# A second SwiGLU whose gate and up projections are seven block products of sums instead of eight

## The chip, the cores and the metric

One core of a Trainium2 chip runs the kernel. Its engines work side by side, each through its own queue and in that queue's order: TensorE multiplies matrices (PE in the profile, its weight loads PEld), VectorE (DVE) and ScalarE (ACT) do arithmetic on 128 partitions, GpSimd (POOL) does the same more slowly, SyncE (SP) issues transfers from memory. TensorE reads operands in SBUF and writes sums into eight PSUM banks of 128x512 numbers. The metric is the time of one execution in microseconds (us). The kernel before takes 2198.51 us, the median of three runs (2197.66 to 2201.56).

## The reference

Two decoder layers over 1024 tokens of width 1024. Layer 0 mixes tokens with a Conformer convolution, layer 1 with dilated attention; after each mixer stands a SwiGLU block of inner width 2816, and at the end an RMS norm. What the change touches is the second of these lines, in layer 1:

```python
x = x + dilated_attention(h, attn_w_qkv[j], attn_w_o[j], rel_bias)
h = rmsnorm(x, norm_ffn[i])
x = x + swiglu(h, ffn_w_gate[i], ffn_w_up[i], ffn_w_down[i])
# swiglu: (silu(h @ w_gate) * (h @ w_up)) @ w_down, all in float32
```

## The kernel before

Everything is kept transposed: features on the 128 partitions, tokens along the free axis, in two halves of 512 tokens (h = 0 and 1). So `x[d][h]` is feature tile d (8 of them) of one half, 128x512.

A float32 product is made of three products in the chip's faster float32r: each operand is split into a rounded high part and the rest as low part, and `gemm` (line 148) issues, for each of the K tiles of 128 inner features, high x high, low x high and high x low (lines 154 to 156). `split` (line 123) makes the parts: a cast on ScalarE (line 126) and a subtraction on VectorE or GpSimd (line 127). For weights, `weights` (line 137) loads a row of 128x1024 into one of two buffers `ws` and splits it into `wh` and `wl` (three buffers each); in layer 1 the subtraction goes to VectorE for every other row and to GpSimd for the rest (`PATTERNS`).

The SwiGLU of layer 1 is run by `ffn`. It goes through groups of four feature tiles (one group has two) out of 22. `ffn_up` makes, for each tile f, a gate product and an up product for each token half: 8 K tiles, so 24 matmuls, into a PSUM tile `mm`. ScalarE applies Silu to the gate (line 259), VectorE multiplies it with the up product (line 265), and the result is split into the group's hidden tile. `ffn_down` multiplies a group's hidden tiles with the down weights into PSUM tiles `aux` and VectorE adds them to x (line 310). The last group is followed, half by half, by the final norm (`final`).

Into this block leads the hand-over from attention. `attn_layer` ends with two calls of `wo_half` (the output projection, added to x at line 837), each followed by `rms_pair`, which makes the normalised operand of one token half: `rstd` sums the squares of the 8 feature tiles (line 196), TensorE turns the result into a row in PSUM, line 207 multiplies each x tile by it, and the 8 products are split. While the second half's operand is made, `AHEAD[1] = 8` lets TensorE do the first 8 gate and up jobs for half 0 alone; the weights of these jobs are loaded and split a second time for half 1.

The order of the instructions on each engine is fixed when the program is built, by a scheduler that goes by the order of the code and by its own estimate of when operands and buffers are there. Nothing is reordered when it runs: an instruction that waits holds up all behind it on its engine.

## Time and profile before

| | |
|---|---|
| median of three runs | 2198.51 us |
| the profiled execution | 2198.14 us |
| its span on the core | 2196.3 us |
| TensorE busy | 2136.2 us, 97% |
| VectorE busy | 1147.2 us, 52% |
| ScalarE busy | 802.0 us, 37% |
| GpSimd busy | 662.2 us, 30% |
[...]

A matmul's busy time in the profile overlaps with the next one's, so a group's busy time divided by its count (389 ns) is not what one costs; the number of matmuls that start in a window says that. Line numbers of the profile are those of the kernel before; in the changed kernel the same lines stand one further down as far as attention.

### The profile page before, as it was taken

The numbers are of one execution on the slowest core, as the hardware profiler recorded it, in microseconds if no ns is written. First come the engines' busy times: TensorE is split into PE (matmuls) and PEld (weight loads), VectorE is DVE, ScalarE is ACT, GpSimd is POOL, SyncE is SP. The second block draws the span as 40 slices with busy tenths as digits, with TensorE's granted clock in tenths as the row PEclk, the third lists the DMA queues.
The fourth block names the chain that finished last, engine by engine and source line by source line (L and its number), as shares of the span: only waits on it lengthen the run. The fifth ranks groups of instructions, "written<-read, shape, count | busy, mean of one in ns | idle before, by whom it ended". The sixth has DMA issues, their size and how long they took to land.

```text
span 2196.3 us, 24621 instructions
## 1 busy us (share of the span) xinstructions
PE 2136.2 (97%) x9832; PEld 1733.7 (79%) x9832; DVE 1147.2 (52%) x1536; ACT 802.0 (37%) x1226; POOL 662.2 (30%) x384
## 2 busy tenths in 40 slices
PE   8998889999999999999999999999999999999998
PEld 6785677778877788888887877778888888888887
DVE  8998597996463333432743355684423232323225
ACT  7666466423433222212434434453212122211114
POOL 3997189811322122210321111142211111111103
PEclk9999999999999999999999999999999999999999
DMA  6111222222323232321231211123312221212212
GB/s 242 49 39 48 68 68 87 87 96 87 106 77 127 92 98 96 102 70 48 87 106 53 73 63 51 59 89 96 97 57 64 71 67 48 87 48 67 67 48 77
DMA packets 54486, 173.66 MB, mean 79 GB/s; under 512 B 6237, under 2 KB 11620, under 8 KB 54372
## 3 DMA queue, kind: packets, MB, share of 16 engines
q1 hardware_dynamic: 52068, 169.21, 23.5%
q10 hardware_dynamic: 2304, 2.88, 0.4%
q8 instruction: 77, 1.26, 0.2%
q14 instruction: 37, 0.30, 0.0%
HBM read 165.51 MB, written 6.55 MB: 78 GB/s over the span
## 4 chain that ended last, share of the span: by engine, by line
PE 78%; DVE 11%; POOL 6%; ACT 2%; DMA 2%; issue 1%; SPq 0%; DVEq 0%; ACTq 0%; POOLq 0%
PE mm L154 17%; PE mm L155 17%; PE mm L156 17%; PE aux L154 7%; PE aux L155 7%; PE aux L156 7%; POOL ap L398 5%; DVE cacc L406 4%; PE att L735 1%; DVE slot L127 1%; PE aux L773 1%; PE aux L765 1%; DVE wl L127 1%; ACT slot L126 1%; DVE ssq L196 1%
## 5 line engine op out<-in xcount | busy, mean ns | idle before, releaser
L154 PE MATMUL mm<-slot,wh 128*128 128x512 f32 x1888 | 742.1, 393 | 10.1 <-ACT slot L126 8.7
L155 PE MATMUL mm<-slot,wl 128*128 128x512 f32 x1888 | 740.1, 392 | 2.1 <-DVE wl L127 2.1
L156 PE MATMUL mm<-slot,wh 128*128 128x512 f32 x1888 | 736.1, 392 | 1.9 <-DVE slot L127 1.2
L127 POOL TENSOR_TENSOR wl<-ws,wh 128x1024 fp32r<-128x1024 f32 (+1 forms) x135 | 321.3, 2380 | 1335.0 <-ACT wh L126 1298.7
L126 ACT CAST wh<-ws 128x1024 fp32r<-128x1024 f32 (+1 forms) x278 | 288.3, 1038 | 593.1 <-PE aux L156 249.7
L154 PEld LDWEIGHTS mm<-slot,wh 128*128 128x128 f32 x1888 | 356.5, 189 | 91.5 <-ACT slot L126 10.4
L155 PEld LDWEIGHTS mm<-slot,wl 128*128 128x128 f32 x1888 | 356.7, 189 | 79.5 <-DVE wl L127 3.2
L156 PEld LDWEIGHTS mm<-slot,wh 128*128 128x128 f32 x1888 | 355.7, 188 | 78.8 <-DVE slot L127 2.4
L127 DVE TENSOR_TENSOR wl<-ws,wh 128x1024 fp32r<-128x1024 f32 (+1 forms) x143 | 184.1, 1288 | 341.9 <-ACT wh L126 326.4
L398 POOL TENSOR_TENSOR ap<-ap,m 128x512 f32<-128x512 f32 x170 | 248.2, 1493 | 44.3 <-ACT m L397 44.2
L154 PE MATMUL aux<-slot,wh 128*128 128x512 f32 x640 | 251.1, 392 | 8.4 <-DVE x L310 8.4
L155 PE MATMUL aux<-slot,wl 128*128 128x512 f32 x640 | 250.5, 391 | 0.5 <-DVE wl L127 0.5
L156 PE MATMUL aux<-slot,wh 128*128 128x512 f32 x640 | 250.2, 391 | 0.0
L310 DVE TENSOR_TENSOR x<-aux,x 128x512 f32<-128x512 f32 (+1 forms) x200 | 133.0, 668 | 173.6 <-PE aux L156 173.3
L406 DVE SCALAR_TENSOR_TENSOR cacc<-u,wd_sb,cacc 128x512 f32<-128x512 f32 x288 | 200.0, 748 | 0.2
L397 ACT ACTIVATE m<-u,wd_sb 128x512 f32<-128x512 f32 x170 | 121.6, 724 | 90.6 <-POOL ap L398 90.5
L154 PEld LDWEIGHTS aux<-slot,wh 128*128 128x128 f32 x640 | 120.8, 189 | 34.2 <-DVE x L310 9.2
L155 PEld LDWEIGHTS aux<-slot,wl 128*128 128x128 f32 x640 | 121.0, 189 | 26.3 <-DVE wl L127 0.9
L156 PEld LDWEIGHTS aux<-slot,wh 128*128 128x128 f32 x640 | 120.8, 189 | 25.3
L127 DVE TENSOR_TENSOR slot<-tmp,slot 128x512 fp32r<-128x512 f32 x66 | 102.0, 1548 | 34.7 <-ACT slot L126 34.4
L265 DVE TENSOR_TENSOR ftmp<-mm,ftmp 128x512 f32<-128x512 f32 x52 | 36.0, 692 | 151.6 <-PE mm L156 151.5
L154 PE MATMUL mm<-slot 128*128 128x512 f32 x256 | 102.5, 400 | 9.4 <-ACT slot L499 6.7
(174 smaller groups left out, 1923.0 us busy)
## 6 DMA issues: line engine op xcount, KB each, us to landing
ws<-wd SPq DMA_DIRECT2D x84, 512.0 KB, 3.4
ws<-wg SPq DMA_DIRECT2D x66, 512.0 KB, 3.4
ws<-wu SPq DMA_DIRECT2D x66, 512.0 KB, 3.4
ws<-w SPq DMA_DIRECT2D x40, 512.0 KB, 3.5
ws<-wqkv SPq DMA_DIRECT2D x34, 512.0 KB, 3.5
ws<-wo SPq DMA_DIRECT2D x16, 384.0 KB, 3.0
x<-xT SPq DMA_DIRECT2D x16, 256.0 KB, 6.1
scratch<-tmp ACTq DMA_DIRECT2D x12, 192.0 KB, 2.0
```

Source lines behind the costliest of these rows:

```text
L126: a = nc.scalar.copy(hi, src)
L127: b = eng.tensor_tensor(out=lo, in0=src, in1=hi.bitcast(F32), op=ALU.subtract)
L154: nc.tensor.matmul(ps, wh[:, sl], xh, start=(k == 0), stop=False)
L155: nc.tensor.matmul(ps, wl[:, sl], xh, start=False, stop=False)
L156: nc.tensor.matmul(ps, wh[:, sl], xl, start=False, stop=(k == kt - 1))
L196: nc.vector.tensor_tensor(out=acc, in0=acc, in1=sq, op=ALU.add)
L265: nc.vector.tensor_tensor(out=t, in0=ps, in1=s, op=ALU.mult)
L310: nc.vector.tensor_tensor(out=x[d][h][:, sl], in0=ps, in1=x[d][h][:, sl], op=ALU.add)
L397: nc.scalar.activation(m, src(c, k), AF.Copy, scale=wk)
L398: nc.gpsimd.tensor_tensor(out=a, in0=a, in1=m, op=ALU.add)
L406: nc.vector.scalar_tensor_tensor(out=a if k or late else u[h, c][:, :TH], in0=src(c, k), scalar=wk, in1=b if k == nv - 1 else a, op0=ALU.mult,
L735: nc.tensor.matmul(s[a][:, pr, c0:], q[rs, pr, us], kb, start=True, stop=True)
```

## The change

Write the product of a pair of feature tiles with all tokens as a 2x2 block product: the weights have two blocks along the features (i, a tile each) and two along the inner dimension (512 features each, a11, a12, a21, a22), the activations two blocks along the inner dimension and two token halves (b11, b12, b21, b22). The plain way takes eight block products of 4 K tiles, 12 matmuls each. The new function `seven_ffn` makes the four results from seven, whose operands are sums: weights a11, a12, a22, s1 = a21 + a22, s2 = s1 - a11, s3 = a11 - a21 and s4 = a12 - s2, and activations b11, b21, b22, t1 = b12 - b11, t2 = b22 - t1, t3 = b22 - b12 and t4 = b21 - t2. `quad` does this for one pair and one projection. Products that go into one result accumulate in one PSUM tile; a partial sum that two results need is copied or added out of PSUM between (u2, u3), and the sinks add it to the other results. `parts` splits each weight operand of 128x512, with the subtraction always on VectorE, into buffers with the tags `wl` and `wh` in turn.

`first_half` makes b11 and b21 while the second `wo_half` runs; `other_half` makes the five operands that need token half 1. `begin` does, for the first two pairs, the two products that need half 0 alone (`AHEAD[1] = 2`), and keeps the value that `quad` goes on with. `down` is the down projection of one pair, for both halves, and stands between the next pair's gate and up quads. The last two pairs share a down projection as before.

```diff
@@ -66,10 +66,11 @@
-AHEAD = (4, 8)
-
-
-TAIL = (256,)
+AHEAD = (4, 2)
+TAILS = (slice(0, 256), slice(256, 512))
 GROUPS = (
-    ((0, 1, 2, 3), (4, 5, 6, 7), (8, 9), (10, 11, 12, 13), (14, 15, 16, 17), (18, 19, 20, 21)),
+    ((0, 1), (2, 3), (4, 5), (6, 7), (8, 9), (10, 11), (12, 13), (14, 15), (16, 17), (18, 19, 20, 21)),
 )
@@ -878,10 +879,235 @@
             todo.append(partial(merged, 1))
             step(STEPS[8])
             wo_half(0, o[0], partial(step, STEPS[9]))
-            out = [rms_pair(0, V_FFN + DC)]
-            wo_half(1, o[1])
-            out.append(rms_pair(1, V_FFN + DC))
-            return out
+        return partial(wo_half, 1, o[1])
+    def seven_ffn(layer, gcol, second_half, ahead):
+        groups = GROUPS[layer]
+        n_pairs = FT // 2
+        H = D // 2
+        with ExitStack() as cs:
...
+            def hid_tile(dtype=F32R):
+                return fpool.tile([P, 2, TH], dtype, tag="hid", name="hid", bufs=4)
...
+            def sub(out, a, b, eng=nc.vector, op=ALU.subtract):
+                eng.tensor_tensor(out=out, in0=a, in1=b, op=op)
+            X = {}
+            def operand(*names):
+                for n in names:
+                    X[n] = slot([P, 2, 4, TH]) if n != "T3" else fpool.tile([P, 2, 4, TH], F32R, name="T3")
+                    nc.vector.tensor_copy(X[n][:, 0, 0, 0:2], ones[:, 0:2])
+            def into(n, k, src, eng=nc.vector):
+                split(src, X[n][:, 0, k], X[n][:, 1, k], eng)
...
+            def first_half():
+                operand("B11", "B21")
+                bc = rstd(lambda c: x[c][0], TH, main)
+                hold = [hid_tile(F32) for _ in range(4)]
+                for c in range(DC):
+                    t = hold[c % 4][:, c // 4]
+                    normed(t, 0, c, gcol, bc, whole)
+                    into("B21" if c // 4 else "B11", c % 4, t, nc.gpsimd if c % 2 else nc.vector)
+                return hold
+            def other_half(hold):
+                operand("T3", "T2", "T1", "B22", "T4")
+                bc = rstd(lambda c: x[c][1], TH, main)
+                for k in range(4):
+                    b11, b21 = hold[k][:, 0], hold[k][:, 1]
+                    b12, t1, b22, t2 = (tmp() for _ in range(4))
+                    normed(b12, 1, k, gcol, bc, whole)
+                    sub(t1, b12, b11)
+                    normed(b22, 1, 4 + k, gcol, bc, whole)
+                    into("B22", k, b22, nc.gpsimd)
+                    sub(t2, b22, t1)
+                    into("T2", k, t2)
+                    t3, t4 = sum_tile(), sum_tile()
+                    sub(t3, b22, b12)
+                    into("T3", k, t3)
+                    into("T1", k, t1)
+                    sub(t4, b21, t2)
+                    into("T4", k, t4)
+            def sum_tile():
+                return fpool.tile([P, TH], F32, tag="sum", name="sum", bufs=3)
+            def product(ps, w, n, start=True):
+                for k in range(4):
+                    sl = slice(k * P, (k + 1) * P)
+                    wh, wl = w[:, 0, sl], w[:, 1, sl]
+                    xh, xl = X[n][:, 0, k], X[n][:, 1, k]
+                    nc.tensor.matmul(ps, wh, xh, start=start and k == 0, stop=False, skip_group_check=not start)
+                    nc.tensor.matmul(ps, wl, xh, start=False, stop=False, skip_group_check=not start)
+                    nc.tensor.matmul(ps, wh, xl, start=False, stop=k == 3, skip_group_check=not start)
...
+            def parts(src):
+                turns["operand"] += 1
+                tag = "wl" if turns["operand"] % 2 else "wh"
+                t = wpool.tile([P, 2, H], F32R, tag=tag, name="wp")
+                split(src, t[:, 0], t[:, 1], nc.vector)
+                return t
+            def begin(ap, sink):
+                r = row(ap)
+                b1 = mm_ps()
+                product(b1, parts(r[:, :H]), "B11")
+                keep = s_tile()
+                nc.scalar.copy(keep, b1)
+                product(b1, parts(r[:, H:]), "B21", False)
+                sink(0, 0, b1, None)
+                return keep
+            def quad(row0, row1, sink, kept=None):
+                r0, r1 = row(row0), row(row1)
+                a11, a12, a21, a22 = (r[:, sl] for r in (r0, r1) for sl in (slice(0, H), slice(H, D)))
+                b1, u2 = None, kept
+                if kept is None:
+                    b1 = mm_ps()
+                    product(b1, parts(a11), "B11")
+                    u2 = tmp()
+                    nc.scalar.copy(u2, b1)
+                s1, s2 = sum_tile(), sum_tile()
+                sub(s1, a21, a22, op=ALU.add)
+                sub(s2, s1, a11)
+                b2 = mm_ps()
+                product(b2, parts(s2), "T2")
+                nc.vector.tensor_tensor(out=u2, in0=b2, in1=u2, op=ALU.add)
+                s3 = sum_tile()
+                sub(s3, a11, a21)
+                b4 = mm_ps()
+                product(b4, parts(s3), "T3")
+                u3 = tmp()
+                nc.vector.tensor_tensor(out=u3, in0=b4, in1=u2, op=ALU.add)
+                b3 = nps_ps()
+                product(b3, parts(s1), "T1")
+                sink(1, 1, b3, u3)
+                if b1 is not None:
+                    product(b1, parts(a12), "B21", False)
+                    sink(0, 0, b1, None)
+                product(b4, parts(a22), "T4", False)
+                sink(1, 0, b4, u2)
+                s4 = sum_tile()
+                sub(s4, a12, s2)
+                product(b3, parts(s4), "B22", False)
+                sink(0, 1, b3, u2)
...
+            def up_sink(s, hid, place, first=False):
+                def hidden(i, h):
+                    t = hid[i, h] = place(i, h)
+                    split(s[i, h], t[:, 0], t[:, 1], nc.vector)
+                if first:
+                    hidden(0, 0)
+                def fn(i, h, ps, u):
+                    t = s[i, h]
+                    if u is None:
+                        sub(t, ps, t, op=ALU.mult)
+                    else:
+                        v = tmp()
+                        sub(v, ps, u, op=ALU.add)
+                        sub(t, v, t, op=ALU.mult)
+                    hidden(i, h)
+                return fn
+            def down(p, hid):
+                for b in range(2):
+                    r = row(wd[layer, 2 * p + b])
+                    for j in range(2):
+                        w = parts(r[:, j * H : (j + 1) * H])
+                        for i in range(2):
+                            d = b * 4 + j * 2 + i
+                            for h in range(2):
+                                ps = aux_ps()
+                                gemm(ps, (w[:, 0], w[:, 1]), lambda k: (hid[k, h][:, 0], hid[k, h][:, 1]), 2, i * 2 * P)
+                                sub(x[d][h], ps, x[d][h], op=ALU.add)
+            hold = first_half()
+            second_half()
+            other_half(hold)
+            gates = [dict() for _ in range(n_pairs)]
+            hids = [dict() for _ in range(n_pairs)]
+            kept = {}
+            for p in range(ahead):
+                kept[p, 0] = begin(wg[layer, 2 * p], gate_sink(gates[p]))
+                kept[p, 1] = begin(wu[layer, 2 * p], up_first(gates[p]))
+            for p in range(n_pairs):
+                last = p == n_pairs - 1
+                quad(wg[layer, 2 * p], wg[layer, 2 * p + 1], gate_sink(gates[p]), kept.get((p, 0)))
+                if 0 < p < n_pairs - 1:
+                    down(p - 1, hids[p - 1])
+                place = lambda i, h: hid_tile()
+                if last:
+                    rest = slot([P, 2, 2, 2, TH])
+                    place = lambda i, h: rest[:, i, h]
+                quad(
+                    wu[layer, 2 * p], wu[layer, 2 * p + 1], up_sink(gates[p], hids[p], place, p < ahead), kept.get((p, 1))
+                )
...
     def final(h, sl, sc):
@@ -904,8 +1130,7 @@
     hs = conv_and_half_ffn()
     hs = ffn(0, NHALF, hs, 0, lambda h, sl, sc: rms_pair(h, V_MIX + DC, sc))
-    hs = attn_layer(hs)
-    ffn(1, 0, hs, AHEAD[1], final, [slice(a, b) for a, b in zip((0,) + TAIL, TAIL + (TH,))])
+    seven_ffn(1, V_FFN + DC, attn_layer(hs), AHEAD[1])
```

Two places of VectorE's queue show what moved. The first is the hand-over, from the point where the statistics of token half 1 are there. Before: line 207 makes the normalised tiles `tmp`, line 127 the low parts of the operand (`slot_10651`), of the first hidden tile (`slot_10731`) and of a weight row (`wl`).

```order
L203 RECIPROCAL rs_10684<-sd_10682 128x4
L265 TENSOR_TENSOR ftmp_10797<-mm_10772,ftmp_10764 128x512
L127 TENSOR_TENSOR slot_10731<-ftmp_10797,slot_10731 128x512
L207 SCALAR_TENSOR_TENSOR tmp_10691<-x0_1_87,vec_76,aux_10686 128x512
L207 SCALAR_TENSOR_TENSOR tmp_10695<-x1_1_89,vec_76,aux_10686 128x512
L207 SCALAR_TENSOR_TENSOR tmp_10699<-x2_1_91,vec_76,aux_10686 128x512
L207 SCALAR_TENSOR_TENSOR tmp_10703<-x3_1_93,vec_76,aux_10686 128x512
L127 TENSOR_TENSOR slot_10651<-tmp_10695,slot_10650 128x512
L207 SCALAR_TENSOR_TENSOR tmp_10707<-x4_1_95,vec_76,aux_10686 128x512
L207 SCALAR_TENSOR_TENSOR tmp_10711<-x5_1_97,vec_76,aux_10686 128x512
L127 TENSOR_TENSOR slot_10651<-tmp_10703,slot_10650 128x512
L207 SCALAR_TENSOR_TENSOR tmp_10715<-x6_1_99,vec_76,aux_10686 128x512
```

After: line 208 makes the normalised tiles, line 914 the sums (`tmp`, `sum`) and line 128 the low parts of T1 (`slot_10658`), T2 (`slot_10656`), T3 and T4 (`slot_10662`), `hid` holds b11.

```order
L204 RECIPROCAL rs_10694<-sd_10692 128x4
L128 TENSOR_TENSOR wp_10919<-ws_10899,wp_10919 128x512
L208 SCALAR_TENSOR_TENSOR tmp_10701<-x0_1_87,vec_76,aux_10696 128x512
L914 TENSOR_TENSOR tmp_10702<-tmp_10701,hid_10418 128x512
L208 SCALAR_TENSOR_TENSOR tmp_10703<-x4_1_95,vec_76,aux_10696 128x512
L914 TENSOR_TENSOR tmp_10704<-tmp_10703,tmp_10702 128x512
L914 TENSOR_TENSOR sum_10713<-tmp_10703,tmp_10701 128x512
L128 TENSOR_TENSOR slot_10658<-tmp_10702,slot_10658 128x512
L914 TENSOR_TENSOR sum_10714<-hid_10418,tmp_10704 128x512
L208 SCALAR_TENSOR_TENSOR tmp_10723<-x1_1_89,vec_76,aux_10696 128x512
L128 TENSOR_TENSOR slot_10656<-tmp_10704,slot_10656 128x512
L128 TENSOR_TENSOR T3_10654<-sum_10713,T3_10654 128x512
```

It goes on like this for the four inner tiles, and ends with the first weight operands, `wp_10944` for s2 and `wp_10981` for s1.

```order
L914 TENSOR_TENSOR sum_10939<-ws_10937 128x512
L128 TENSOR_TENSOR slot_10656<-tmp_10770,slot_10656 128x512
L128 TENSOR_TENSOR T3_10654<-sum_10779,T3_10654 128x512
L128 TENSOR_TENSOR slot_10662<-sum_10780,slot_10662 128x512
L914 TENSOR_TENSOR sum_10940<-sum_10939,ws_10935 128x512
L914 TENSOR_TENSOR sum_10960<-ws_10935,ws_10937 128x512
L128 TENSOR_TENSOR wp_10944<-sum_10940,wp_10944 128x512
L128 TENSOR_TENSOR wp_10981<-sum_10939,wp_10981 128x512
```

From the first of line 208 to the low part `wp_10944` stand 47 instructions now, 8 of them of line 208; TensorE's next instruction behind the `begin` products reads `wp_10944`. In the same place the eight of line 207 stood with four low parts on VectorE (the other four on GpSimd).

The second place is the start of a down projection in the middle of the layer. Before, the additions to x (line 310) stand with the low parts of weight rows between them.

```order
L265 TENSOR_TENSOR ftmp_11273<-mm_11248,ftmp_11240 128x512
L127 TENSOR_TENSOR slot_10732<-ftmp_11273,slot_10732 128x512
L310 TENSOR_TENSOR x0_0_86<-aux_11283,x0_0_86 128x512
L310 TENSOR_TENSOR x1_0_88<-aux_11297,x1_0_88 128x512
L127 TENSOR_TENSOR wl_11382<-ws_11379,wh_11381 128x1024
L310 TENSOR_TENSOR x2_0_90<-aux_11317,x2_0_90 128x512
L310 TENSOR_TENSOR x3_0_92<-aux_11331,x3_0_92 128x512
L310 TENSOR_TENSOR x4_0_94<-aux_11351,x4_0_94 128x512
L310 TENSOR_TENSOR x5_0_96<-aux_11365,x5_0_96 128x512
```

After, for a pair in the middle: the down projection's last weight operand (`wp_12615`), the next up quad's first one (`wp_12655`, from the rows `ws_12650` and `ws_12652`), its sums, the ends of the gate quad (`s`), and then the first addition to x.

```order
L128 TENSOR_TENSOR wp_12615<-ws_12578,wp_12615 128x512
L914 TENSOR_TENSOR s_12483<-mm_12414,tmp_12389 128x512
L128 TENSOR_TENSOR wp_12655<-ws_12650,wp_12655 128x512
L914 TENSOR_TENSOR sum_12672<-ws_12652 128x512
L914 TENSOR_TENSOR s_12503<-nps_12432,tmp_12389 128x512
L914 TENSOR_TENSOR sum_12673<-sum_12672,ws_12650 128x512
L914 TENSOR_TENSOR sum_12693<-ws_12650,ws_12652 128x512
L914 TENSOR_TENSOR x0_0_86<-aux_12511,x0_0_86 128x512
L128 TENSOR_TENSOR wp_12677<-sum_12673,wp_12677 128x512
L914 TENSOR_TENSOR x0_1_87<-aux_12519,x0_1_87 128x512
```

The first addition to x now stands behind four instructions that read the up quad's two weight rows. Over one pair in the middle VectorE has 60 instructions of 128x512, 16 for the gate quad, 24 for the up quad and 20 for the down projection.

## Rows read from the trace of the kernel before

**Rows 1.** which engines are busy, over the whole span: engine, busy us (share), instructions
```profile
PE 2136.2 (97%) x9832; PEld 1733.7 (79%) x9832; DVE 1147.2 (52%) x1536; ACT 802.0 (37%) x1226; POOL 662.2 (30%) x384
```

**Rows 2.** the chain that ended last, by engine, over the whole span
```profile
PE 78%; DVE 11%; POOL 6%; ACT 2%; DMA 2%; issue 1%; SPq 0%; DVEq 0%; ACTq 0%; POOLq 0%
```

**Rows 3.** windows in the second layer's SwiGLU: length, then busy us (xcount) per engine
```profile
core 0: us, PE busy (x) PEld busy (x) DVE busy (x) ACT busy (x) POOL busy (x), PEclk, DMA share, GB/s
1500.00:1550.00 50.00, 50.00 (x222) 41.42 (x221) 19.11 (x14) 13.96 (x18) 9.58 (x4) 1.00 0.32 100
1800.00:1850.00 50.00, 50.00 (x223) 41.39 (x222) 13.07 (x12) 10.20 (x14) 4.79 (x2) 1.00 0.17 54
2050.00:2100.00 50.00, 50.00 (x223) 41.39 (x222) 12.24 (x11) 9.72 (x13) 7.18 (x3) 1.00 0.17 53
```

**Rows 4.** groups by line and form, 1500 to 2100 us
```profile
L156 PE MATMUL mm<-slot,wh 128*128 128x512 f32 x595 | 231.5, 389 | 0.0
...
L156 PE MATMUL aux<-slot,wh 128*128 128x512 f32 x288 | 112.0, 389 | 0.0
...
L127 POOL TENSOR_TENSOR wl<-ws,wh 128x1024 fp32r<-128x1024 f32 x39 | 93.4, 2394 | 504.9 <-ACT wh L126 504.9
...
L127 DVE TENSOR_TENSOR slot<-ftmp,slot 128x512 fp32r<-128x512 f32 x38 | 65.2, 1715 | 30.6 <-ACT slot L126 30.6
L310 DVE TENSOR_TENSOR x<-aux,x 128x512 f32<-128x512 f32 x80 | 55.1, 690 | 99.6 <-PE aux L156 99.6
...
L126 ACT CAST slot<-ftmp 128x512 fp32r<-128x512 f32 x37 | 22.8, 616 | 73.4 <-DVE ftmp L265 73.4
L259 ACT ACTIVATE ftmp<-mm 128x512 f32<-128x512 f32 x37 | 22.2, 601 | 157.6 <-PE mm L156 157.6
```

**Rows 5.** VectorE's timeline at the hand-over: start us, us, instruction [idle before]
```profile
1454.78 2.89 DVE L196 TENSOR_TENSOR ssq<-ssq,tmp 128x512 f32<-128x512 f32 x1
1457.59 0.68 DVE L837 TENSOR_TENSOR x<-mm,x 128x512 f32<-128x512 f32 x1
1458.19 0.68 DVE L127 TENSOR_TENSOR slot<-tmp,slot 128x512 fp32r<-128x512 f32 x1
1458.79 1.48 DVE L196 TENSOR_TENSOR ssq<-ssq,tmp 128x512 f32<-128x512 f32 x2
...
1475.06 2.52 DVE L127 TENSOR_TENSOR slot<-ftmp,slot 128x512 fp32r<-128x512 f32 x1 [0.95 <-ACT slot L126]
1477.50 2.71 DVE L207 SCALAR_TENSOR_TENSOR tmp<-x,vec,aux 128x512 f32<-128x512 f32 x4
```

**Rows 6.** GpSimd's timeline in the same stretch
```profile
1453.01 1.30 POOL L127 TENSOR_TENSOR slot<-tmp,slot 128x512 fp32r<-128x512 f32 x1 [1.26 <-ACT slot L126]
1454.26 2.86 POOL L127 TENSOR_TENSOR wl<-ws,wh 128x1024 fp32r<-128x1024 f32 x1
...
1474.64 2.39 POOL L127 TENSOR_TENSOR wl<-ws,wh 128x1024 fp32r<-128x1024 f32 x1 [9.19 <-ACT wh L126]
```

**Rows 7.** what TensorE waited for, 1400 to 2197 us, the longest
```profile
PE mm L155 <- DVE wl L127: 2.1, 1, 2.1
PE mm L176 <- DVE fssq L196: 1.9, 1, 1.9
```

**Rows 8.** windows before, in and after TensorE's short stop (PEclk, then DMA share, GB/s, last)
```profile
1415.00:1420.00 5.00, 3.60 (x14) 1.99 (x13) 4.91 (x8) 2.90 (x5) 1.82 (x1) 1.00 0.25 80
1420.00:1425.00 5.00, 4.99 (x15) 3.44 (x15) 4.67 (x8) 1.28 (x3) 1.46 (x2) 0.66 0.24 79
1430.00:1435.00 5.00, 5.00 (x24) 4.14 (x23) 4.46 (x7) 2.40 (x4) 1.81 (x1) 1.00 0.01 2
```

**Rows 9.** weight loads: queue, count, size, median us from issue to landing
```profile
ws<-wg SPq DMA_DIRECT2D x66, 512.0 KB, 3.4
```

**Rows 10.** TensorE's timeline at the kernel's end
```profile
2187.87 0.60 PE L176 MATMUL mm<-ones,fssq 128*128 128x1 f32 x4 [1.90 <-DVE fssq L196]
```

More of the change, by code (lines that the diff above doesn't have):

```diff
@@ L880, in attn_layer, with f32, nps_ps, s_tile @@
             wo_half(0, o[0], partial(step, STEPS[9]))
-            out = [rms_pair(0, V_FFN + DC)]
-            wo_half(1, o[1])
-            out.append(rms_pair(1, V_FFN + DC))
-            return out
+        return partial(wo_half, 1, o[1])
[4 more added lines that the diff above has]
+        with ExitStack() as cs:
+            nps = cs.enter_context(tc.tile_pool(name="nps", bufs=2, space=PS))
+            fpool = cs.enter_context(tc.tile_pool(name="fpool", bufs=1))
+            turns = {"operand": 0}
+            def f32(ap):
+                return ap.bitcast(F32)
+            def nps_ps():
+                return nps.tile([P, TH], F32, tag="nps", name="nps")
+            def hid_tile(dtype=F32R):
+                return fpool.tile([P, 2, TH], dtype, tag="hid", name="hid", bufs=4)
+            def s_tile():
+                return fpool.tile([P, TH], F32, tag="s", name="s", bufs=6)
+            def sub(out, a, b, eng=nc.vector, op=ALU.subtract):
[7 more added lines that the diff above has]
+                split(src, X[n][:, 0, k], X[n][:, 1, k], eng)
+            whole = slice(0, TH)
+            def first_half():
[35 more added lines that the diff above has]
+                    nc.tensor.matmul(ps, wh, xl, start=False, stop=k == 3, skip_group_check=not start)
+            def row(ap):
+                r = wpool.tile([P, D], F32, tag="ws", name="ws", bufs=2)
+                nc.sync.dma_start(r, ap)
+                return r
+            def parts(src):
[46 more added lines that the diff above has]
+                sink(0, 1, b3, u2)
+            def gate_sink(s):
+                def fn(i, h, ps, u):
+                    t = s[i, h] = s_tile()
+                    if u is None:
+                        nc.scalar.activation(t, ps, AF.Silu)
+                    else:
+                        sub(t, ps, u, op=ALU.add)
+                        nc.scalar.activation(t, t, AF.Silu)
+                return fn
+            def up_first(s):
+                def fn(i, h, ps, u):
+                    sub(s[i, h], ps, s[i, h], op=ALU.mult)
+                return fn
+            def up_sink(s, hid, place, first=False):
[4 more added lines that the diff above has]
+                    hidden(0, 0)
+                def fn(i, h, ps, u):
+                    t = s[i, h]
+                    if u is None:
+                        sub(t, ps, t, op=ALU.mult)
+                    else:
+                        v = tmp()
+                        sub(v, ps, u, op=ALU.add)
+                        sub(t, v, t, op=ALU.mult)
+                    hidden(i, h)
+                return fn
+            def down(p, hid):
[30 more added lines that the diff above has]
+                )
+            gi = len(groups) - 1
+            ws = down_weights(layer, gi)
+            sc = Scratch(tpool, "tmp", fpool, "s", nps_ps)
+            sc.acc = sc.out = s_tile
+            four = {(j, h): hids[n_pairs - 2 + j // 2][j % 2, h] for j in range(4) for h in range(2)}
+            for h in range(2):
+                for sl in TAILS if h else (slice(0, TH),):
+                    for d in range(DC):
+                        ps = aux_ps()[:, : sl.stop - sl.start]
+                        gemm(ps, ws[d // 2], lambda k: (four[k, h][:, 0, sl], four[k, h][:, 1, sl]), 4, d % 2 * 4 * P)
+                        nc.vector.tensor_tensor(out=x[d][h][:, sl], in0=ps, in1=x[d][h][:, sl], op=ALU.add)
+                    final(h, sl, sc)
```

## The prediction

> **What bounds the kernel now.** I read the shares of the engines first. TensorE is busy for 97% of the span, VectorE for 52%, ScalarE for 37%, GpSimd for 30% [rows 1], and the chain that ended last runs through TensorE for 78% [rows 2]. Shares over the whole span hide stages, so I then cut the stage of the change into windows: from 1500 to 2100 us TensorE has no idle time, at the full granted clock, while VectorE is busy for a quarter to two fifths [rows 3]. In this stage time is the number of matmuls times the distance between two starts. The distance is not the 389 ns that a group gives as mean, because neighbours overlap: 3 x 595 + 3 x 288 = 2649 matmuls start in 600 us [rows 4], 0.2265 us each. What TensorE waits for from 1400 us on is little: 2.1 us for a weight's low part in the hand-over from attention and 1.9 us for the last sum of squares [rows 7].
>
> So a matmul less in this stage is 0.2265 us less, as long as the other engines, which get more to do, deliver in time. There are three places to look at: the stage itself, its first microseconds, and its end.
>
> **Matmuls removed.** Gate and up of 22 tiles for two halves were 22 x 2 x 2 x 24 = 2112 matmuls. Now 11 pairs x 2 projections x 7 products x 12 = 1848. The down projection keeps its 1056. That is 264 fewer, all 128x512: 264 x 0.2265 = **59.8 us** less TensorE time.
>
> **VectorE in the middle of the stage.** A pair in the middle gives TensorE 168 + 96 = 264 matmuls, 59.8 us by chance the same number. VectorE has 60 instructions per pair. What one costs depends on GpSimd: undisturbed ones start 0.60 us apart (1457.59, 1458.19, 1458.79) with a duration of 0.68 [rows 5], and those that read PSUM have a mean of 0.69 [rows 4]. Where GpSimd works, an instruction with both inputs in SBUF stands until GpSimd is through: the one of 1454.78 took 2.89 us and ended at 1457.67, just after GpSimd's of 1454.26 ended at 1457.12; the one of 1475.06 took 2.52 us beside GpSimd's of 1474.64 [rows 5, 6]. This makes the 1.715 us of the hidden tile's low part before [rows 4]. The pairs give GpSimd nothing, so I take 0.60 to 0.69: 36 to 41 us of 59.8. ScalarE has 22 casts, 2 copies and 4 Silus per pair, 28 x 0.62 = 17 us [rows 4]. By load both are hidden behind TensorE.
>
> Load is not enough, since VectorE's queue is in order. Its tightest place is the start of a down projection, where the first addition to x frees the PSUM tile that the down projection's fourth result takes (there are three), and stands behind sums of the next two weight rows. Their transfer can be issued only when the down projection's last weight part has been read out of the buffer. From the product whose Silu stands ahead of that cast on ScalarE to the down projection's fourth result TensorE has 54 matmuls, 12.2 us. In it must go: Silu 0.60, cast 0.62, low part 0.60, transfer 3.4 and the second row's issue behind the first's, some 0.3, five VectorE instructions 3.0 [rows 4, 5, 9]: 8.5 us. That leaves 3.7 us, and it is the smallest margin that I count in the pairs. I add nothing for them.
>
> **The hand-over.** Here it doesn't fit. Once the statistics of token half 1 stand in PSUM, the kernel before had 139 of the 192 matmuls of its eight early jobs left, 31.5 us, for eight normalised tiles and their parts. Now 48 of the 96 matmuls of `begin` are left, 48 x 0.2265 = 10.9 us, and then TensorE needs the low part of s2, which is the 47th VectorE instruction. Eight of these are normalisations, four in 2.71 us [rows 5], 8 x 0.68 = 5.4 us. The other 39 cost 39 x 0.60 = 23.4 us. GpSimd makes the four low parts of b22 in this stretch, 1.30 us each [rows 6]; all four in the way would be 5.2 us, none 0, and I take 4.0 because most of the 47 have both inputs in SBUF. Instructions that need the result of the one just ahead may wait a little: two such additions took 1.48 us [rows 5], 0.2 more than two free ones; for some four of them 0.8 us. Sum 33.6 us, minus 10.9: TensorE stands for **22.7 us**. The bounds are 18 (none of the two extras) and 32 (5.2, and 0.2 for each of the 47).
>
> [...]
>
> [...]
>
> Right behind the restart TensorE's second matmul needs the next low part, one VectorE instruction later: **0.6 us**. After that each product of 12 matmuls (2.7 us) needs about two and a half VectorE instructions (1.5 us), so VectorE gets ahead again.
>
> **The end and the rest.** The last group's down projection and the final norm keep their form, with 1.9 us of waiting for the last sum of squares [rows 7, 10]; I add nothing, with 1 us to either side. The weights of the eight early jobs are no longer loaded and split twice. That was off the path.
>
> **Sum.** -59.8 + 22.7 + 2.0 + 0.6 = -34.5. The profiled execution took 2198.14 us (span 2196.3 and 1.8 around it), the median of the runs is 2198.51, 0.4 above. 2198.1 - 34.5 = 2163.6, so **2164 us**. With the bounds of the hand-over alone (18.0 + 0.6 at least, 32 + 4 + 0.6 at most, and 1 for the end) it is 2156 to 2176.
>
> **Rivals.**
> 1. The hand-over is cheaper. If half of its VectorE work were done earlier, the stop would be 33.6 / 2 - 10.9 = 6 us and the time 2198.1 - 59.8 + 6 + 2 = 2146. For it speaks that the stage before has VectorE time to spare. Against it: all 47 instructions need the statistics that TensorE itself puts into PSUM ahead of the 48 matmuls, and the first weight operand stands last in the queue.
> 2. Each pair waits. Two rows of 512 KB are now asked for at once, and the 3.4 us of landing [rows 9] is for rows that came one by one. If both landed 5.7 us later than counted, the margin of 3.7 is gone by 2 us in each of nine pairs: 18 us, 2182. Against it: the transfer engines are busy for 13 to 32% in this stage [rows 3], room for both.
> 3. Slower: VectorE becomes the bound of the pairs. This decides once an instruction takes on average more than (59.8 + 34.5 / 9) / 60 = 1.06 us. At 1.08 a pair takes 64.8 us, nine pairs lose 45, and the time is 2209. For it speak the 1.715 us that a low part takes now [rows 4]; against it, that these stood beside GpSimd's 39 subtractions of 2.394 us, and that none of those is left.
> That the change doesn't do what it says would show as a distance between matmuls other than 0.2265 us; shape and operand layout are the same, and no row speaks for it.
>
> **How the numbers follow.** The forecast has 0.64 and its own range is 2156 to 2176. The cheaper hand-over has 0.09, pairs that wait 0.19 (most of it below 2190, a little within 0.2% of the time before), slower 0.08 with what I have not thought of. The range of 2150 to 2182 leaves out about 0.2: the cheapest hand-overs below, the upper half of rival 2 and rival 3 above. Differences under 0.2%, 4 us, are about what a measurement of this kernel can't tell from none (its three runs span 3.9 us). Faster by more than that 0.90, within 0.03, slower 0.07.
>
> **What would show it.** In the profile after, windows in the middle of the pairs have TensorE at 50 of 50 us with 222 or 223 matmuls, GpSimd at 0 and VectorE near 0.65; matmuls start 0.2265 us apart. At the hand-over TensorE has one wait of about 23 us for a low part `wp`, with a granted clock of about half right behind it, and 47 VectorE instructions from the first normalisation to that low part in about 34 us. No wait of TensorE inside the pairs is above 1 us. If windows of pairs show TensorE idle, rival 2 (a wait for an `aux` tile behind a transfer) or 3 (VectorE at 1.0) holds; if the hand-over's stop is under 15 us or over 33 us, its term is wrong.

## The result: faster by 24.5 us where 34.5 were forecast

The changed kernel takes 2174.7 us (median of 4 runs, 2173.0 to 2177.3) against 2199.2 before (4 runs): ratio 0.9889, 95% interval 0.9872 to 0.9906. The direction is right and the time lies in the range of 2150 to 2182, but ten of the 34.5 us are missing. The profiled execution took 2172.99 us, 25.15 less than the one before.

The page of the kernel after, as [rows 1, 2]: busy us (share) and instructions by engine, then the chain that ended last.

```profile
PE 2087.4 (96%) x9568; PEld 1684.9 (78%) x9568; DVE 1356.6 (62%) x1975; ACT 843.8 (39%) x1360; POOL 559.9 (26%) x340
...
PE 76%; DVE 11%; POOL 6%; issue 3%; ACT 2%; DMA 1%; SPq 0%; POOLq 0%; DVEq 0%; ACTq 0%
```

TensorE has exactly 264 instructions fewer than in [rows 1] and still carries the chain. Now the windows of the pairs, as [rows 3]:

```profile
1550.00:1600.00 50.00, 50.00 (x218) 40.72 (x217) 33.42 (x53) 14.29 (x24) 0.00 (x0) 1.00 0.16 53
1800.00:1850.00 50.00, 50.00 (x220) 40.75 (x219) 32.69 (x51) 15.08 (x25) 0.00 (x0) 1.00 0.17 54
2050.00:2100.00 50.00, 50.00 (x220) 40.93 (x219) 31.91 (x49) 15.05 (x25) 0.00 (x0) 1.00 0.15 52
```

TensorE is busy for all of it at the full granted clock, VectorE for 0.64 to 0.67, GpSimd not at all: as forecast. But 218 to 220 matmuls start in 50 us, not 222 or 223. Each has become 1 to 2% dearer, with no wait to show for it. TensorE's waits from 1400 us on (total, times, longest) hold none inside the pairs. As [rows 7, 10]:

```profile
PE mm L967 <- ACT wp L127: 18.7, 1, 18.7
PE mm L177 <- DVE s L197: 3.6, 2, 3.3
PE mm L967 <- ACT s L990: 2.0, 1, 2.0
PE aux L155 <- DVE x L1109: 1.8, 2, 1.2
PE mm L156 <- DVE wl L128: 1.8, 1, 1.8
```

The first and the third are the hand-over (L967 to L969 are the products' matmuls, `mm` and `nps` their PSUM tiles, L990 is the copy in `begin`), the second and the fourth stand in the last group and the final norm, and the fifth lies before 1470 us, ahead of the hand-over. Behind 2100 us the kernel before had, beside the 1.9 us of [rows 7] and a wait of 0.6 us that both kernels have:

```profile
PE aux L154 <- DVE x L310: 0.3, 1, 0.3
```

**Where the distance grew.** One product on T3 from TensorE's timeline (start us, duration), its first and last matmul:

```profile
1651.40 0.39 PE L967 MATMUL mm<-T,wp 128*128 128x512 f32 x1
...
1653.96 0.40 PE L969 MATMUL mm<-T,wp 128*128 128x512 f32 x1
```

Twelve matmuls have eleven distances: 2.56 / 11 = 0.2327 us. Averaged over the starts of 1560 to 2110 us in the same way, matmuls that stream T3 or a hidden tile stand 0.2333 us apart, those that stream a slot 0.2276. Before, all streamed slots, at 0.2267. The duration (0.39) shows nothing of this. What the slow ones share is the pool: T3 and the hidden tiles lie in `fpool`, all else that the products stream in slots.

**The hand-over.** VectorE's timeline, as [rows 5]: the first normalisation, the four stretched instructions, and the first weight's low part.

```profile
1474.03 0.74 DVE L208 SCALAR_TENSOR_TENSOR tmp<-x,vec,aux 128x512 f32<-128x512 f32 x1
...
1477.41 1.78 DVE L128 TENSOR_TENSOR slot<-tmp,slot 128x512 fp32r<-128x512 f32 x1
...
1487.71 1.10 DVE L128 TENSOR_TENSOR slot<-tmp,slot 128x512 fp32r<-128x512 f32 x1
...
1494.86 1.10 DVE L128 TENSOR_TENSOR slot<-tmp,slot 128x512 fp32r<-128x512 f32 x1
...
1499.55 1.75 DVE L914 TENSOR_TENSOR sum<-tmp 128x512 f32<-128x512 f32 x1
...
1505.65 1.90 DVE L128 TENSOR_TENSOR wp<-sum,wp 128x512 fp32r<-128x512 f32 x3
```

With the first normalisation 46 instructions stand ahead of the low part, which is the 47th; it starts 31.6 us after the first, and forecast were 33.6 for all 47. The stretched ones overlap with GpSimd's four subtractions, which start at 1476.95, 1485.00, 1492.60 and 1499.15 and take 1.60 to 3.26 us. Not every instruction with both inputs in SBUF stood until GpSimd was through: those of 1485.25, 1485.85 and 1486.45 took 0.68 us each beside GpSimd's of 1485.00, which took 3.26. TensorE's timeline shows the two stops and the restart:

```profile
1483.94 0.50 PE L967 MATMUL mm<-slot,wp 128*128 128x512 f32 x1 [1.96 <-ACT s L990]
...
1505.67 0.80 PE L967 MATMUL mm<-slot,wp 128*128 128x512 f32 x1 [18.72 <-ACT wp L127]
1506.26 0.72 PE L967 MATMUL nps<-slot,wp 128*128 128x512 f32 x1
1506.78 0.63 PE L968 MATMUL mm<-slot,wp 128*128 128x512 f32 x1
1507.21 0.63 PE L969 MATMUL mm<-slot,wp 128*128 128x512 f32 x1
...
1510.09 0.39 PE L967 MATMUL mm<-slot,wp 128*128 128x512 f32 x1
1510.31 0.39 PE L968 MATMUL mm<-slot,wp 128*128 128x512 f32 x1
```

The long stop ends with the high part of s2, ScalarE's cast (L127), and not with the low part that the prediction named; the low part is needed one matmul later. After the stop most starts are 0.43 us apart until 1510, then 0.23. The windows around it (granted clock is the third number from the end), as [rows 8]:

```profile
1500.00:1505.00 5.00, 0.00 (x0) 0.00 (x0) 5.00 (x8) 1.50 (x4) 0.75 (x1) 0.50 0.00 0
1505.00:1510.00 5.00, 4.33 (x10) 3.36 (x11) 4.30 (x7) 2.79 (x5) 0.00 (x0) 0.51 0.17 32
1510.00:1515.00 5.00, 5.00 (x23) 4.03 (x23) 2.62 (x4) 0.43 (x1) 0.00 (x0) 1.00 0.44 179
```

The granted clock is 0.50 of full from 1500 to 1505 us, 0.51 from 1505 to 1510 and 1.00 from 1510 on. The ten matmuls from 1505.67 to 1510.09 took 4.42 us, at 0.2267 they would have taken 2.27.

ScalarE's timeline shows where the first stop came from, the 1.96 us before 1483.94, and what the cast at the end of the long one waited for:

```profile
1482.30 0.62 ACT L127 CAST hid<-s 128x512 fp32r<-128x512 f32 x1 [1.84 <-DVE s L914]
1482.82 0.59 ACT L1033 ACTIVATE s<-mm 128x512 f32<-128x512 f32 x1
1483.31 0.58 ACT L990 COPY s<-mm 128x512 f32<-128x512 f32 x1
...
1505.00 1.66 ACT L127 CAST wp<-sum 128x512 fp32r<-128x512 f32 x3 [2.45 <-DVE sum L914]
```

The copy that TensorE waits for first stands in ScalarE's queue behind a cast that waits for a product of VectorE. The cast at 1505.00 starts right behind VectorE's sum for s2 (1504.23, 0.68 us), after 2.45 us in which ScalarE had nothing to do: both stops go back to VectorE's queue.

### The profile page after: what moved, and what is told of

Read it like the earlier page. It is cut to its first block, busy times and chain, and to the rows that moved or that the text cites. A ratio compares the mean times of both kernels' runs of the same rounds, so it can differ in the third digit from the quotient of the medians.

```text
span 2171.2 us, 24611 instructions
## 1 busy us (share of the span) xinstructions
PE 2087.4 (96%) x9568; PEld 1684.9 (78%) x9568; DVE 1356.6 (62%) x1975; ACT 843.8 (39%) x1360; POOL 559.9 (26%) x340
## 4 chain that ended last, share of the span: by engine, by line
PE 76%; DVE 11%; POOL 6%; issue 3%; ACT 2%; DMA 1%; SPq 0%; POOLq 0%; DVEq 0%; ACTq 0%
PE mm L155 11%; PE mm L156 11%; PE mm L157 11%; PE aux L155 6%; PE aux L157 6%; PE aux L156 6%; POOL ap L399 5%; PE mm L967 4%; PE mm L968 4%; PE mm L969 4%; DVE cacc L407 4%; PE nps L967 2%; PE nps L968 2%; PE nps L969 2%; DVE slot L128 2%
## 5 line engine op out<-in xcount | busy, mean ns | idle before, releaser
L155 PE MATMUL mm<-slot,wh 128*128 128x512 f32 x1184 | 468.5, 396 | 10.1 <-ACT slot L127 8.7
L156 PE MATMUL mm<-slot,wl 128*128 128x512 f32 x1184 | 466.5, 394 | 2.0 <-DVE wl L128 2.0
L157 PE MATMUL mm<-slot,wh 128*128 128x512 f32 x1184 | 462.5, 393 | 1.9 <-DVE slot L128 1.2
L128 POOL TENSOR_TENSOR wl<-ws,wh 128x1024 fp32r<-128x1024 f32 (+1 forms) x91 | 215.0, 2363 | 809.2 <-ACT wh L127 777.9
L127 ACT CAST wh<-ws 128x1024 fp32r<-128x1024 f32 (+1 forms) x190 | 195.4, 1030 | 341.3 <-PE mm L157 167.3
L155 PEld LDWEIGHTS mm<-slot,wh 128*128 128x128 f32 x1184 | 224.6, 190 | 63.9 <-ACT slot L127 10.4
L156 PEld LDWEIGHTS mm<-slot,wl 128*128 128x128 f32 x1184 | 224.6, 190 | 51.8 <-DVE wl L128 3.0
L157 PEld LDWEIGHTS mm<-slot,wh 128*128 128x128 f32 x1184 | 223.6, 189 | 51.1 <-DVE slot L128 2.2
L967 PE MATMUL mm<-slot,wp 128*128 128x512 f32 x352 | 138.4, 393 | 20.7 <-ACT wp L127 18.7
L155 PE MATMUL aux<-slot,wh 128*128 128x512 f32 x352 | 139.1, 395 | 8.4 <-DVE x L311 8.4
L156 PE MATMUL aux<-slot,wl 128*128 128x512 f32 x352 | 138.6, 394 | 0.5 <-DVE wl L128 0.5
L157 PE MATMUL aux<-slot,wh 128*128 128x512 f32 x352 | 138.2, 393 | 0.0
L968 PE MATMUL mm<-slot,wp 128*128 128x512 f32 x352 | 138.1, 392 | 0.0
L969 PE MATMUL mm<-slot,wp 128*128 128x512 f32 x352 | 137.9, 392 | 0.0
L914 DVE TENSOR_TENSOR x<-aux,x 128x512 f32<-128x512 f32 x144 | 98.7, 688 | 39.1 <-PE aux L157 38.3
L127 ACT CAST wp<-ws 128x512 fp32r<-128x512 f32 x102 | 63.1, 621 | 145.2 <-PE mm L969 46.1
```

What stands on the lines that cost most here:

```text
L127: a = nc.scalar.copy(hi, src)
L128: b = eng.tensor_tensor(out=lo, in0=src, in1=hi.bitcast(F32), op=ALU.subtract)
L155: nc.tensor.matmul(ps, wh[:, sl], xh, start=(k == 0), stop=False)
L156: nc.tensor.matmul(ps, wl[:, sl], xh, start=False, stop=False)
L157: nc.tensor.matmul(ps, wh[:, sl], xl, start=False, stop=(k == kt - 1))
L914: eng.tensor_tensor(out=out, in0=a, in1=b, op=op)
```

## Experiments: which distance, and why

A tile's start is given here modulo 256 bytes. Slots and weight tiles start 32 bytes past a 256-byte line, `fpool` 224 past one; every tile in them is a multiple of 256 bytes long, so all T3 and hidden tiles stand at 224. All kernels up to e6 have the changed kernel's order of instructions.

**e1: move `fpool` alone.**
```diff
             fpool = cs.enter_context(tc.tile_pool(name="fpool", bufs=1))
+            fpool.tile([P, 16], F32, name="pad")
```


> Edit: one 64-byte tile ahead of the first tile of fpool, nothing else. T3 and the hidden tiles start 64 bytes later, so that they stand to a 256-byte line as the slots do (32 bytes past it, where it was 224). The order on the engines stays. Theory of the address's place in a line: the matmuls whose moving operand is hid or T3 (864 of the down projections, 96 of the last group, 264 products of T3) go from 0.2333 us between starts to the slots' 0.2275, about 7 us off the changed kernel's 2174.7, to about 2167.5. Theory of the region (high addresses are slower) and theory of contention with VectorE's and ScalarE's work beside the matmuls: distances stay at 0.233, time within 2 us of 2174.7.

**e3: move slots and weights, leave `fpool`.**
```diff
+    spool = ctx.enter_context(tc.tile_pool(name="spool", bufs=2))
     slots = ctx.enter_context(tc.tile_pool(name="slots", bufs=6))
...
-    spool = ctx.enter_context(tc.tile_pool(name="spool", bufs=2))
```


> Edit: the pool of the small row-norm tiles (192 bytes) is opened ahead of the slots, so that the slots and the weight tiles lie 192 bytes higher, 224 bytes past a 256-byte line, as hid and T3 do; fpool stays where it is. Theory of the address's place in a line: every matmul on a slot goes from about 0.2266 to 0.2275 us between starts to about 0.233, some 6,000 to 7,500 matmuls by 0.006, 36 to 45 us slower: about 2215. Theory of the region or of contention: no change, 2174.7 within 2 us.

**e4: everything on a line.**
```diff
-    const = ctx.enter_context(tc.tile_pool(name="const", bufs=1))
-    xpool = ctx.enter_context(tc.tile_pool(name="xpool", bufs=1))
+    rpool = ctx.enter_context(tc.tile_pool(name="rpool", bufs=2))
...
     tpool = ctx.enter_context(tc.tile_pool(name="tpool", bufs=4))
+    const = ctx.enter_context(tc.tile_pool(name="const", bufs=1))
+    xpool = ctx.enter_context(tc.tile_pool(name="xpool", bufs=1))
...
-        sd = spool.tile([P, 4], F32, name="sd")
+        sd = rpool.tile([P, 4], F32, name="sd")
...
-        rs = spool.tile([P, 4], F32, name="rs")
+        rs = rpool.tile([P, 4], F32, name="rs")
...
+            fpool.tile([P, 8], F32, name="pad")
```


> Edit: the pools are opened in another order and fpool gets a first tile of 32 bytes, so that slots, weight tiles, hid and T3 all start on a 256-byte line (the order on the engines stays). Theory of the address's place in a line: all matmuls of 128x512 have one distance; if 32 bytes past a line costs a part of what 224 costs, it falls below 0.2266, and with 8,000 matmuls each 0.001 us is 8 us: 2160 or lower; if 32 past is as good as 0, hid and T3 alone gain, about 2167. Theory of the region: slots now lie from 768 on, lower than before, hid and T3 stay high: no change, 2174.7 within 2 us. Theory of contention: no change.

All three came out alike, and this felled my first theory: e3 made nothing slow, though it moved every slot to 224. Not the place of one operand matters, then. In all three the streamed operand and the weights stand *alike* to the line. Two theories remained, and the next two runs separate them.

**e5: the changed kernel again.** 

> The changed kernel once more, word for word, on the chip of this series. After the three runs before (all three at 0.2266 us between starts and 2167 to 2168 us, also the one that left hid and T3 where they were) two theories stand. Theory of the pair (a matmul is slow where its moving operand and its weights stand differently to a 256-byte line; in the three runs they stand alike): 0.2333 us again for hid and T3, 2174.7 within 2 us. Theory of the execution (the distance belongs to the chip or the run and not to an address): 0.2266 us everywhere and 2167 to 2168 us.

**e6: move the weights alone.**
```diff
     slots = ctx.enter_context(tc.tile_pool(name="slots", bufs=6))
+    spool = ctx.enter_context(tc.tile_pool(name="spool", bufs=2))
     wpool = ctx.enter_context(tc.tile_pool(name="wpool", bufs=3))
...
-    spool = ctx.enter_context(tc.tile_pool(name="spool", bufs=2))
```


> Edit: the pool of the small row-norm tiles (192 bytes) is opened between the slots and the weight tiles. Slots stay at 32 bytes past a 256-byte line, weight tiles go to 224, hid and T3 stay at 224. Theory of the pair: now the matmuls on slots are the slow ones, in the whole kernel some 6,000 by 0.006 us, while hid and T3 come down to 0.2266: 2174.7 + 36 - 8 = about 2203. Theory of the execution: 0.2266 everywhere, 2167 to 2168.

| kernel | slots / weights / fpool, bytes past a line | us | ratio to before (95%) |
|---|---|---|---|
| after | 32 / 32 / 224 | 2174.7 | 0.9889 (0.9872 to 0.9906) |
| e5 | 32 / 32 / 224 | 2174.3 | 0.9883 (0.9866 to 0.9901) |
| e1 | 32 / 32 / 32 | 2168.0 | 0.9852 (0.9837 to 0.9867) |
| e3 | 224 / 224 / 224 | 2168.2 | 0.9851 (0.9836 to 0.9866) |
| e4 | 0 / 0 / 0 | 2166.9 | 0.9852 (0.9835 to 0.9868) |
| e6 | 32 / 224 / 224 | 2184.4 | 0.9924 (0.9908 to 0.9940) |

The same window of each kernel's trace, 550 us in the SwiGLU. Before, after, and e5:

```profile
1550.00:2100.00 550.00, 550.00 (x2429) 455.40 (x2428) 171.66 (x180) 108.88 (x134) 83.78 (x35) 1.00 0.21 66
```

```profile
1550.00:2100.00 550.00, 550.00 (x2391) 448.18 (x2390) 353.22 (x545) 153.45 (x254) 0.00 (x0) 1.00 0.16 52
```
```profile
1550.00:2100.00 550.00, 550.00 (x2391) 447.94 (x2390) 353.79 (x545) 153.47 (x254) 0.00 (x0) 1.00 0.16 52
```
e1, and e6:
```profile
1550.00:2100.00 550.00, 550.00 (x2428) 455.59 (x2427) 357.09 (x551) 155.01 (x257) 0.00 (x0) 1.00 0.17 53
```
```profile
1550.00:2100.00 550.00, 550.00 (x2402) 450.58 (x2401) 359.32 (x555) 155.72 (x259) 0.00 (x0) 1.00 0.16 52
```

e3 and e4 also have 2428. The 37 matmuls between 2391 and 2428 are the loss, and e5 has it to the matmul: it belongs to the kernel, not to an execution. e6 is 10 us slower than the changed kernel, as the theory of the pair says in sign, but not by the 28 expected: hidden tiles and T3, now like their weights, came down to 0.2286 and 0.2278, slots rose to 0.2297, not to 0.2333. That left the size of the effect open, so I measured it by itself.

**e8: the distance alone.** One tile of weights, one streamed tile, 60 matmuls per case, one execution; in all cases but the last few only the first byte of the streamed operand changes. Beside them VectorE makes six copies out of PSUM; ScalarE and GpSimd do nothing.
```diff
+            xh = mov[:, 0, dh // 4 : dh // 4 + TH]
+            xl = mov[:, 1, dl // 4 : dl // 4 + TH]
...
+            nc.tensor.matmul(ps, w, m, start=i == 0, stop=i == len(ops) - 1)
```


> No part of the reference is computed: one tile of weights and one moving tile, both at the same place in a 256-byte line, and TensorE alone at work with 60 matmuls of 128x512 in a row for each case, in the order of the kernel's products (high weights by high part, low weights by high part, high weights by low part). The cases differ in how many bytes past the tile's start the moving operand begins. Theory of the pair: the distance between starts depends on moving less weights: 0.2267 us at 0, 256, 512 and 1024 bytes, 0.2333 at 192 and 448, 0.229 at 64 (as 224 less 32, and 32 less 224, gave); 32, 96, 128, 160 and the small ones are open, and one below 0.2267 would be worth 0.001 us x 8,000 matmuls = 8 us each 0.001. Rival (the distance is made by the other engines' reads and writes beside the matmuls): 0.2267 in every case.

TensorE's timeline of e8, one row per case (start us, us). Cases d, h, j, n begin 64, 192, 256 and 1024 bytes past the weights' place, o 16 bytes; in r the streamed high part begins 64 bytes past it and the low part at it:

```profile
60.22 13.66 PE L47 MATMUL cased<-mov,wp 128*128 128x512 f32 x59
73.72 14.17 PE L47 MATMUL casee<-mov,wp 128*128 128x512 f32 x60
...
115.79 14.16 PE L47 MATMUL caseh<-mov,wp 128*128 128x512 f32 x60
129.78 14.16 PE L47 MATMUL casei<-mov,wp 128*128 128x512 f32 x60
143.78 13.79 PE L47 MATMUL casej<-mov,wp 128*128 128x512 f32 x60
157.40 14.15 PE L47 MATMUL casek<-mov,wp 128*128 128x512 f32 x60
...
199.01 13.76 PE L47 MATMUL casen<-mov,wp 128*128 128x512 f32 x60
212.61 14.06 PE L47 MATMUL caseo<-mov,wp 128*128 128x512 f32 x60
226.51 14.18 PE L47 MATMUL casep<-mov,wp 128*128 128x512 f32 x60
...
254.15 14.16 PE L47 MATMUL caser<-mov,wp 128*128 128x512 f32 x60
268.15 14.07 PE L47 MATMUL cases<-mov,wp 128*128 128x512 f32 x60
```

From one start to the next: d (73.72 - 60.22) / 59 = 0.2288 us; h 13.99 / 60 = 0.2332; j 0.2270; n 0.2267; o 0.2317; r 14.00 / 60 = 0.2333. Taken over each case like this, and without case a, the first, the distances are 0.2266 to 0.2270 for 0, 256, 512 and 1024 bytes, 0.2288 for 64, 0.2317 for 16, and 0.2332 to 0.2343 for 8, 32, 96, 128, 160, 192, 224, 384 and 448. Shifting only the high part, only the low part, only the high weights, or all but the low weights by 64 gave 0.2333, 0.2318, 0.2313 and 0.2312. So where all products of a stream stand alike, the distance goes with the streamed operand's start less the weights', modulo 256, and no other engine is needed for it. That does not cover all cases: in the first, second and fourth of these mixed ones every matmul stands at 0 or 64 bytes, and yet the distances lie above 0.2288, so the places of neighbouring matmuls count too. Why the place matters is not shown. The cases fit the sizes: the changed kernel's `fpool` stands at 192 (0.2332 here, 0.2333 measured there), and e6's slots at 32 - 224, which is 64 modulo 256 (0.2288, not 0.2333). No case of these is below 0.2266. After a change of operand the starts stay uneven for about five matmuls: in the changed kernel's trace the first five distances on slots behind T3 or a hidden tile average 0.227, 0.235, 0.229, 0.231 and 0.230, those from the sixth on 0.2267. That is why slots, unmoved, came to 0.2276: they alternate with tiles at 192.

**e9: an eighth product again,** on e1: is each matmul worth its distance?
```diff
-                product(b2, parts(s2), "T2")
+                w2 = parts(s2)
+                product(b2, w2, "T2")
+                product(b2, w2, "T2")
```


> Edit, on the kernel with the 64-byte tile ahead of fpool: the product on T2 is computed twice into the same tile, with the same weights, so that each of the 22 quads has eight products again (264 matmuls more), while VectorE, ScalarE and the DMAs do what they did. Theory of the prediction (in the pairs TensorE alone sets the time, each matmul is worth its distance, and no wait hides behind): 264 x 0.22667 = 59.8 us more, 2168.0 + 59.8 = 2227.8. Rival (part of the pairs' time is set by VectorE or by hand-offs, so that the eighth product falls partly into waits): 10 us or more below that, under 2218.

2225.7 us, ratio 1.0119 (1.0104 to 1.0134), 57.7 above e1 and, by the ratios, (1.0119 - 0.9852) x 2200 = 58.7. The starts stay as close as in e1: 2428 matmuls from 1550 to 2100 us. e1's four runs spread from 2165.2 to 2171.5, so 59.8 is not told apart from this; the rival's 10 us less are excluded. In the traces the stretch from the restart behind the long stop to the end is 60.0 us longer than e1's (719.0 against 659.0). It also says that, the distance mended, eight products in this frame would be slower than the kernel before.

**e7: the hand-over in another order,** on e1. T1 and T4 are kept whole in the buffers of the held tiles; `later` splits T1 behind the first weight operand and T4 behind the second (`turns["ins"]` is the split of the weight operand made last). The scheduler is also told to put the first weight operand's sums and parts early, in lines not shown here.
```diff
-                    b11, b21 = hold[k][:, 0], hold[k][:, 1]
-                    b12, t1, b22, t2 = (tmp() for _ in range(4))
...
+                        t1, t4 = hold[k][:, 0], hold[k][:, 1]
+                        b12, b22, t2 = (tmp() for _ in range(3))
...
-                    into("T1", k, t1)
-                    sub(t4, b21, t2)
-                    into("T4", k, t4)
+                        sub(t4, t4, t2)
...
+                def later(n, i):
+                    a, b = turns["ins"]
+                    with tc.issue_after(a), tc.issue_after(b):
+                        for k in range(4):
+                            into(n, k, hold[k][:, i])
```


> Edit, on the kernel with the 64-byte tile ahead of fpool: in the hand-over the low parts of T1 and T4 (8 of VectorE's instructions) come after the first weight operand, so that 38 stand between the reciprocal and it in place of 47, and the two parts are made beside the first two products. Theory of the step of the prediction (the stop lasts as long as VectorE's instructions to the first weight operand take, less the matmuls beside them): 9 x 0.6 = 5.4 us off the stop of 17.6 us, about 12, and under 1 us of new waits behind it, as five VectorE instructions (3.0 us) stand beside a product of 2.7 us: 2168.0 - 4.5 = about 2163.5. Rival (the stop is set by ScalarE's casts and copies, which keep their number): stop stays at 17 to 18 us, 2168.

2164.1 us, ratio 0.9838 (0.9820 to 0.9855). The waits of e1, and of e7:

```profile
PE mm L968 <- ACT wp L127: 17.6, 1, 17.6
...
PE mm L968 <- ACT s L991: 1.9, 1, 1.9
```
```profile
PE mm L975 <- ACT wp L127: 12.7, 1, 12.7
...
PE mm L976 <- DVE wp L128: 1.5, 1, 1.5
...
PE mm L975 <- ACT s L998: 1.2, 1, 1.2
PE mm L975 <- DVE tmp L1026: 0.9, 1, 0.9
```

Nine instructions fewer ahead of the weight operand took 4.9 us off the stop; new waits behind it came to 2.1 us, not under 1. This alone does not exclude the rival, because eight casts of ScalarE moved behind the first weight operand too. The changed kernel's timeline above does: ScalarE waited 2.45 us for VectorE's sum before it could make the cast that ended the stop. By the medians e7 is 3.9 us under e1, though their intervals overlap; it is the fastest version run here.

**e10: GpSimd out of the hand-over,** on e1.
```diff
-                    into("B22", k, b22, nc.gpsimd)
+                    into("B22", k, b22)
```


> Edit, on the kernel with the 64-byte tile ahead of fpool: the low parts of B22 are made by VectorE in place of GpSimd (4 of 128x512). It tests the term of 4.0 us for GpSimd's four subtractions beside VectorE's. Prediction's prices: 4 x 0.60 = 2.4 us more work, 4.0 less standing still, the stop of 17.6 us becomes 16.0 and the time 2166.4. By the four stretched VectorE instructions of the changed kernel's trace (1.78, 1.10, 1.10 and 1.75 us, 3.3 us over 4 x 0.60): 16.7 and 2167.1. Rival (GpSimd costs VectorE nothing there): stop 20.0, time 2170.4.

50 instructions in 31.1 us, none above 0.9: 0.623 each. At that rate the changed kernel's 46 are 28.6 of 31.6, so GpSimd cost 3.0 us there by this estimate, against 4.0 in the sum; in e1, where the low part starts 30.5 us after the first normalisation, it is 1.9. The stops were 19.0 + 1.2 in place of 17.6 + 1.9, 0.7 more, and the time 2166.5 (0.9829 to 0.9862), not told apart from e1. The trade is about even: neither of the two figures, nor the rival's 20.0.

## Why the prediction was right in sign and ten short

- **Matmuls removed, -59.8:** right. 264 are gone, and e9 prices 264 at 57.7 to 58.7, by the traces 60.0.
- **The distance of 0.2265: the step that failed.** The prediction set aside that it could change, since "shape and operand layout are the same, and no row speaks for it". Shape and layout are the same; the address is not. From the starts after the restart: 912 matmuls on hidden tiles at 0.0066 too much, 264 on T3 at 0.0067, 1536 on slots at 0.0009: 6.0 + 1.8 + 1.4 = **9.2 us**, which the sum had at 0. e1, which changes only that, is 6.7 faster by the medians, 8.1 by the ratios (0.9889 - 0.9852); from the restart to the end its trace is 6.6 shorter than that of the changed kernel and 8.4 shorter than e5's. So 9.2 may be a little too much.
- **VectorE in the pairs, 0:** right, no wait of TensorE there. None of the three rivals came; the stop of rival 1 would have been 6 us.
- **The hand-over, 22.7:** 18.7 + 2.0 = 20.7. The mechanism is the one named, an in-order queue of 47 instructions; e7 shows it by cutting the queue. TensorE restarted behind the cast of s2, whose sum is the 45th instruction, some 0.7 us before the 47th, the low part, was through. GpSimd was 3.0, not 4.0. Not foreseen was the first of the two stops: a matmul of `begin` waits 1.96 us for ScalarE's copy, held up in its queue by VectorE. It adds nothing to the sum, since VectorE's queue sets when TensorE restarts.
- **Clock and second low part, 2.0 + 0.6:** no run shows the 2.0, or the 4 in the upper bound, as a cost of such a stop; the 2.0 was the author's estimate from [rows 8], where 15 matmuls start in 5 us in place of 24 at a granted clock of 0.66: 9 x 0.2265. The trace after has, for both terms together, 4.42 - 2.27 = 2.2.
- **The end, 0 with 1 to either side:** too small. The waits of the last stretch are 3.6 + 1.8, where before had 1.9 [rows 7] and 0.3: 3.2 us more. What causes them was not tried, so it stays open.

Sum: -59.8 + 9.2 + 20.7 + 2.2 + 3.2 = -24.5; measured -25.15. The terms for the hand-over erred on the dear side by 2.4, so the miss on the distance is nearly the whole of it. That 2174.7 still lies within 2156 to 2176 is luck: the upper part of that range stood for a longer stop, and what filled it was a term set at nothing.

## What to carry to other kernels

Where a stage is bound by TensorE, a change that puts streamed operands into another pool changes their address too: keep operand and weights at the same place modulo 256 bytes, one pad tile of 64 bytes was worth 7 to 8 us of 2175 here. Look for it in the count of matmuls per window, since neither waits nor the granted clock (1.00) showed it, and the mean duration hardly (0.390 us on slots, 0.394 on hidden tiles). And an operand that opens a phase should have as few foreign instructions as possible ahead of it in an in-order queue: nine fewer took 4.9 us off the stop here, 2.1 of which came back as new waits.

## What was not expected of the hardware

float32r matmuls of 128x512 with new weights each time start 0.2266 to 0.2270 us apart, averaged over a case of e8 behind its first, when streamed operand and weights all start alike modulo 256 bytes, and 0.2288 to 0.2343 in every other case, with hardly anything but TensorE at work and a mean granted clock of 1.0. Steps of 256, 512 and 1024 bytes gave 0.2270, 0.2270 and 0.2267, as 0 bytes did, and the place of both together to the line made no difference either: at 0, 32 and 224 past it (e4, e1, e3) 2428 matmuls start in the same 550 us.
